# Fixed places for eight additions in a layer's opening, and a new order of its latent statistics

## The chip, the cores and the metric

The kernel runs on one core of one Trainium2 chip. The metric is the time of one execution on the device in microseconds. The kernel before took 889.29 us, the median of three runs (886.87, 889.29 and 890.32). One more execution was profiled: it took 887.62 us, and its profile spans 885.8 us of them.

The engines are named as in the profile: PE is TensorE (matmul), DVE is VectorE, ACT is ScalarE, POOL is GpSimd, SP is SyncE, which only issues transfers here.

## The reference

One decoder layer on x of 512 tokens by 2048, all in float32. Eight heads of latent attention (MLA) and eight forgetting heads (FoX) stand side by side behind one input projection.

```python
h = _rms_norm(x, g_pre)
proj = h @ w_in
(q_lat, kv_lat, k_rope_raw, gate_mla,
 fq, fk, fv, f_logit, gate_fox) = jnp.split(proj, split_points, axis=-1)
# MLA: q = rms_norm(q_lat) @ w_uq; k, v from rms_norm(kv_lat) @ w_ukv; rotary parts
# FoX: c = cumsum(log_sigmoid(f_logit + b_forget)); logits = q k * scale + c_q - c_k
o_mla = _mla_branch(q_lat, kv_lat, k_rope_raw, g_q, w_uq, g_kv, w_ukv, cos, sin) * jax.nn.silu(gate_mla)
o_fox = _fox_branch(fq, fk, fv, f_logit, b_forget) * jax.nn.silu(gate_fox)
o = jnp.concatenate([o_mla, o_fox], axis=-1) @ w_out
return x + _rms_norm(o, g_post)
```

The latents q_lat (768 wide) and kv_lat (512 wide) are normalised over their width, so each needs a sum of squares per token, a root, and a factor per token.

## The kernel before

**Precision.** Every float32 operand is held as two parts, hi (rounded) and lo (the rest), and a product is three matmuls: hi by hi, hi by lo, lo by hi (`mm3`, lines 152 to 154). Of x's tiles the parts are `hh` and `hl` ("h" in the profile). Of a weight they are `whi`, cast by ACT (line 290), and `wlo`, subtracted by DVE (line 291), for each chunk of up to 128 by 1024 numbers. The raw chunk is loaded by SP's queue (`raw`) or POOL's (`rawv`, `rawg`, `rawl`).

**Opening.** x comes in as tokens by width and is turned tile by tile (16 tiles of 128 columns): `x_turn(k)` (line 537) has four transposes on PE into one bank ("xt"), ACT's scaling for the hi part (line 144) and DVE's subtraction for the lo part (line 145). The loop of `proj_first` multiplies tile k with the first chunks of weights (line 655, banks "in"), two tiles to a chunk from the third chunk on. After tile k it turns the next ones: singly for k below 2, then two at a time after each even k. ACT also squares x here (line 550), for the norm of x. The opening is under a manual schedule: PE, ACT and DVE run what `proj_first` holds in the order in which it is written.

**Everything behind.** Outside of it a scheduler orders the instructions of each engine by its own estimate of when they can run; each engine then runs its list strictly in order. Side work (statistics, splits, copies, sums) stands in a queue `todo`, from which the loops over matmuls take a step now and then; `wait(n)` puts n empty steps into it.

**Sums of x.** Products are done in blocks after Strassen's manner, which need sums and differences of x's four quarters. `x_steps(j)` makes those of pair j of tiles (j = 0 to 3): four additions hh + hl into the buffers "xr" (line 1128), then, put at the head of `todo`, `away_steps`: subtractions "rmg" (line 1027), a split "smg", and stores "awaymg" to DRAM by POOL's queue. Later products fetch them ("bmg", SP's queue).

**Forget gates.** `forget_sums` yields steps `fs`. The last of them turn the rows ("rf"), copy them (line 852), scan them (line 858, "fz") and store the result: "c_dram", line 859, by SP's queue. The row of x's norm factors, `make_row(rrow)`, is two matmuls (lines 580, 581) and a copy (582); "fqr" (line 1142) are the first queries times that row.

**Latents.** `latent(i)` copies tile i of the latents and sums its squares (banks "la", "lg", "mg" are of the products that make them). `stats_steps(j)` makes the factors for j = 1 (kv) and j = 0 (q): `mean` (matmuls with ones, "lbk" and "lbq", line 1495), `root`, `steps` and `ends`. `latent_row` turns the factors into a row ("lrk", then the copy "ls"), with which the latents are scaled (line 1532) and split ("ln").

**Up products and heads.** The keys' and values' up product runs on sums of latents that `operand_steps("u", ...)` splits: "suq", "sug"; its banks are uA, uC, uB, uG. For each of four pairs of heads `mla_q` makes three banks mq, splits two of them (lines 141 and 142), copies the first 128 columns of both whole to "mw" by ACT (`whole_block`, line 126: the first block's scores are computed from whole float32), and rotates the third. `mla_k` does likewise for the keys (banks "mk"), which share banks in rotation with those of mq.

Of the kernel before, what the change touches and what calls it, by code (L numbers as in the profile page):

```python
# [19 lines left out]
P = 128  # L20
# [45 lines left out]
def tile_hybrid_layer(  # L66
# [39 lines left out]
    def proj_bank(name):  # L106
        return bank("pj", name, 4)
# [336 lines left out]
    for n in ("q0", "p1", "k0", "q6", "p2", "p4", "g7", "q1", "g5", "k1", "g3", "q2", "k2", "q3", "k3"):  # L444
# [5 lines left out]
        p = int(n[1])  # L450
# [181 lines left out]
    def proj_first(rng, banks):  # L632

        squares = deque(range(2 * NK))
        make_gcol(gains, 0, NK)
        x_turn(0, lambda: prepare(0))
        k = 0
        for i in rng:
            hi, lo = chunk(i, ahead=0)
            n = chunks[i][4]  # L640
            for j in range(chunks[i][3]):
# [19 lines left out]

                for turn in (k + 2,) if k < 2 else () if k % 2 else (k + 2, k + 3):
                    if turn < NK:
                        x_turn(turn)
                if k < 4 and k % 2 == 0:
                    prepare(rng[k // 2 + 2])
                for _ in range(3 if k > 2 and k % 2 else 2):
                    if squares:
                        x_square(squares.popleft())
                k += 1  # L670

# [447 lines left out]

    def x_steps(j):  # L1120

        pair = []

        def whole(h, i):
            if not pair:
                pair.extend(v_block(f"xr{n}{j}") for n in range(2))
            k = 2 * j + 8 * h + i
            dve.tensor_tensor(out=pair[h][:, i, :], in0=hh[k].bitcast(F32), in1=hl[k].bitcast(F32), op=ALU.add)
            if h and i:
                todo.extendleft(reversed(away_steps("m", j, pair, keep="g5")))  # L1130

        return [lambda h=h, i=i: whole(h, i) for h in range(2) for i in range(2)]


# [128 lines left out]
    def two_of(make, name):  # L1263
        return [make(f"{name}{i}") for i in range(2)]

    vb = [proj_bank(f"in{t}") for t in range(NT)]
    with tc.manual_schedule(engines={mybir.EngineType.Activation, mybir.EngineType.DVE, mybir.EngineType.PE}):
# [16 lines left out]
    wait(1)  # L1284
    todo.extend([*x_steps(0), *fs[3:], *x_steps(1)])
    places = [(g, j) for g in "vg" for j in range(4)]
# [5 lines left out]
    drain()  # L1292
    todo.extend([*x_steps(2), *x_steps(3)])

# [191 lines left out]
    def stats_steps(j):  # L1486
# [16 lines left out]

        def root():
            act.sqrt(w, v)

        def steps():
            dve.reciprocal(y, w)
            newton_rsqrt(y, v, w)
            if j == 0:  # L1510
                for to, scale in ((qcol, SC_M), (nqcol, -SC_M)):
                    dve.scalar_tensor_tensor(out=to, in0=y, scalar=scale, in1=rcol, op0=ALU.mult, op1=ALU.mult)
                return
            dve.tensor_tensor(out=y, in0=y, in1=rcol, op=ALU.mult)
# [4 lines left out]

        return [mean, root, steps, ends]  # L1520

# [56 lines left out]
    def first_latents():  # L1578
        wait(2)
        todo.extend(lambda i=i: latent(i, raw(i)) for i in (6, 7, 4, 5))  # L1580
        todo.extend(lambda i=i: latent_part(i) for i in (4, 5))
        todo.extend(s1)
        todo.append(lambda: latent_row(1))
        todo.extend(lambda i=i: latent_part(i) for i in range(6, 10))
# [17 lines left out]
    todo.extend(lambda i=i: latent(i, raw(i)) for i in range(4))  # L1602
    wait(3)
    todo.append(lambda: latent_stats(0))

# [17 lines left out]
    todo.append(lambda: k_parts.extend(zip(*(latents[i] for i in range(6, 10)))))  # L1623
    todo.extend(operand_steps("u", 0, (raws_of[4], raws_of[0]), ("sums",), tmp, part_slot))

# [17 lines left out]
    def mla_q(p):  # L1643

        qb = [proj_bank(f"mq{p}{i}") for i in range(3)]
        proj_T(mla[p]["q"], [(qb[i], P, cols(i * P)) for i in range(3)], qnh, qnl, 2, 6)
        q = [[split(qb[i], f"mq{p}{i}", first=P)] for i in range(2)]
        wholes = slot(f"mw{p}")
        qw = [[whole_block(wholes, i, qb[i])] for i in range(2)]
        a, b = rotate(qb[2], P, 1.0, f"q{p}")  # L1650
# [299 lines left out]
```

## Time and profile before

| | us |
|---|---|
| median of three runs | 889.29 |
| profiled execution | 887.62 |
| its span | 885.8 |
| PE busy | 874.8 |
| DVE busy | 628.6 |
| ACT busy | 503.3 |
| POOL busy | 125.2 |

A busy share says how full an engine is over the whole span; what a change of order is worth is read at the place where an engine waits. A row of the timeline gives start, duration (both in us), engine, line, operation, output and inputs, a shape, and how many like it stand together; in brackets stand the idle time just before it and what ended that. Two matmuls overlap in the pipe, so the distance of two starts, rather than a duration, is what one costs. PE's granted clock was 0.997 of full speed.

### The profile page before, as it was taken

To read this page: it belongs to the slowest core of one execution; us is meant where nothing else is said; L and a number is where in the kernel's file an instruction comes from. 1 tells how busy PE (TensorE), PEld (TensorE's weight loads), DVE (VectorE), ACT (ScalarE), POOL (GpSimd) and SP (SyncE) were. 2 spreads that over 40 slices of the span, in tenths; PEclk is the share of its full clock that TensorE was granted. 3 is DMA by queue.
4 is the path that set the end of the run, shared out by engine and by line. 5 is a ranking of instruction groups with operands and counts; after the bars stand their busy time and mean duration, and the time that the engine had idled before them with its cause. 6 is when DMAs were issued, how large, how long until landed. Compare 5 with 4: busy or idle time off the path is not lost.

```text
span 885.8 us, 13760 instructions
## 1 busy us (share of the span) xinstructions
PE 874.8 (99%) x5078; PEld 772.4 (87%) x5078; DVE 628.6 (71%) x1059; ACT 503.3 (57%) x919; POOL 125.2 (14%) x132
## 2 busy tenths in 40 slices
PE   9999999999999999999999999999999999999996
PEld 9989999999888888889999999988888788888885
DVE  4779466667475644547577677899778777988785
ACT  6844444444167553535654445649685986645383
POOL 0024004450110101000014432100000000000021
PEclk9999999999999999999999999999999999999998
DMA  9499869998597888884799999986969537699878
GB/s 295 146 356 241 274 196 202 228 229 228 87 214 213 223 209 234 228 233 125 248 306 229 236 216 252 207 225 158 222 146 274 121 133 248 203 330 321 260 216 250
DMA packets 128488, 198.41 MB, mean 224 GB/s; under 512 B 16338, under 2 KB 61292, under 8 KB 127396
## 3 DMA queue, kind: packets, MB, share of 16 engines
q1 hardware_dynamic: 101428, 136.28, 49.1%
q0 software_dynamic: 26256, 61.02, 35.2%
q8 instruction: 40, 0.66, 0.3%
q10 hardware_dynamic: 736, 0.22, 0.1%
q14 instruction: 28, 0.23, 0.1%
HBM read 182.60 MB, written 44.25 MB: 256 GB/s over the span
## 4 chain that ended last, share of the span: by engine, by line
PE 85%; DVE 6%; DMA 4%; ACT 3%; issue 1%; SPq 1%; DVEq 0%; ACTq 0%
PE fq L152 3%; PE fk L152 3%; PE fk L154 3%; PE fq L154 3%; PE fk L153 3%; PE fq L153 3%; PE in L655 3%; PE sm L698 2%; DVE wlo L291 2%; PE sf L698 2%; PE oa L153 2%; PE oa L154 2%; PE oa L152 2%; PE od L153 1%; PE od L154 1%; DMA rawl<-in_w_in_dram 1%
## 5 line engine op out<-in xcount | busy, mean ns | idle before, releaser
L291 DVE TENSOR_TENSOR wlo<-raw,whi 128x1024 fp32r<-128x1024 f32 (+3 forms) x159 | 186.7, 1176 | 95.8 <-ACT whi L290 94.6
L290 ACT CAST whi<-raw 128x1024 fp32r<-128x1024 f32 (+3 forms) x159 | 160.4, 1013 | 156.6 <-PE fk L153 43.2
L152 PE MATMUL fk<-h,whi 128*128 128x512 f32 x128 | 51.4, 401 | 0.0
L152 PE MATMUL fq<-h,whi 128*128 128x512 f32 x128 | 50.4, 394 | 0.0
L154 PE MATMUL fk<-h,wlo 128*128 128x512 f32 x128 | 50.1, 392 | 0.0
L154 PE MATMUL fq<-h,wlo 128*128 128x512 f32 x128 | 50.1, 391 | 0.0
L153 PE MATMUL fq<-h,whi 128*128 128x512 f32 x128 | 50.0, 391 | 0.0
L153 PE MATMUL fk<-h,whi 128*128 128x512 f32 x128 | 49.9, 390 | 0.0
L290 ACT CAST whi<-rawv 128x1024 fp32r<-128x1024 f32 x24 | 25.2, 1050 | 43.3 <-PE gg L153 11.0
L290 ACT CAST whi<-rawl 128x1024 fp32r<-128x1024 f32 x25 | 26.2, 1048 | 34.7 <-PE mc L153 7.9
L291 DVE TENSOR_TENSOR wlo<-rawl,whi 128x1024 fp32r<-128x1024 f32 x25 | 30.5, 1224 | 21.7 <-ACT whi L290 21.4
L291 DVE TENSOR_TENSOR wlo<-rawv,whi 128x1024 fp32r<-128x1024 f32 x24 | 29.3, 1224 | 23.1 <-ACT whi L290 23.1
L290 ACT CAST whi<-rawg 128x1024 fp32r<-128x1024 f32 x24 | 25.2, 1052 | 30.6 <-PE vc L154 8.4
L291 DVE TENSOR_TENSOR wlo<-rawg,whi 128x1024 fp32r<-128x1024 f32 x24 | 29.3, 1222 | 13.9 <-ACT whi L290 13.9
L1770 POOL DMA_DIRECT2D c<-in_x_dram x8 | 7.0, 1014 | 171.1 <-ACT c L1769 171.1
L718 ACT ACTIVATE pf<-pf,stf 128x128 f32<-128x128 f32 (+3 forms) x32 | 17.9, 559 | 22.5 <-DVE stf L709 22.5
L243 POOL DMA_DIRECT2D rawl<-in_w_in_dram x20 | 23.8, 1194 | 43.6 <-DVE wlo L291 32.0
L655 PE MATMUL in<-whi,h 128*128 128x328 f32 x128 | 29.1, 319 | 0.0
L152 PE MATMUL mq<-ln,whi 128*128 128x512 f32 x72 | 28.9, 402 | 0.0
L154 PEld LDWEIGHTS fk<-h,wlo 128*128 128x128 f32 x128 | 24.0, 188 | 5.3
L154 PEld LDWEIGHTS fq<-h,wlo 128*128 128x128 f32 x128 | 24.0, 188 | 5.2
L153 PE MATMUL mq<-ln,whi 128*128 128x512 f32 x72 | 28.2, 392 | 0.0
(628 smaller groups left out, 2916.1 us busy)
## 6 DMA issues: line engine op xcount, KB each, us to landing
raw<-in_w_in_dram SPq DMA_DIRECT2D x62, 512.0 KB
raw<-in_w_out_dram SPq DMA_DIRECT2D x32, 512.0 KB
rawl<-in_w_in_dram POOLq DMA_DIRECT2D x20, 512.0 KB, 11.3
rawv<-in_w_in_dram POOLq DMA_DIRECT2D x16, 512.0 KB, 8.1
rawg<-in_w_in_dram POOLq DMA_DIRECT2D x16, 512.0 KB, 8.8
raw<-in_w_in_dram POOLq DMA_DIRECT2D x12, 512.0 KB, 10.2
bmg<-awaymg SPq DMA_DIRECT2D x20, 256.0 KB
rawl<-in_w_in_dram SPq DMA_DIRECT2D x10, 512.0 KB
```

What stands on the lines that cost most here:

```text
L152: pe.matmul(o, ah, bh, start=first, stop=False, **kw)
L153: pe.matmul(o, ah, bl, start=False, stop=False, **kw)
L154: pe.matmul(o, al, bh, start=False, stop=last, **kw)
L243: pool.dma_start(to, second, accum_op=ALU.add)
L290: act.copy(hi[:, :m], raw[:, :m])
L291: dve.tensor_tensor(out=lo[:, :m], in0=raw[:, :m], in1=hi[:, :m].bitcast(F32), op=ALU.subtract)
L655: pe.matmul(banks[t][:, :n], a[k][:, tss[t]], b[:, j, :], start=k == 0 and m == 0, stop=k == NK - 1 and m == 2,)
L698: m = pe.matmul(s[:, :nn], a[:, qs], c[:, :nn], start=(i == 0), stop=(i == len(pairs) - 1))
L718: act.activation(p, p, AF.Exp, bias=st[:, 0:1], scale=unit, accum_out=st[:, 1:2])
L1770: pool.dma_start(to, x[piece(t, c)], accum_op=ALU.add)
```

## The change

It has four parts.

1. Opening: tiles 4 and 5 are turned singly (k below 4 instead of below 2), so that the sixth tile's transposes come after the next tile's matmuls.
2. The eight additions of pairs 0 and 1 (`x_wholes`) get fixed places in the manual schedule: one after each of tiles 10 to 13 and two after each of tiles 14 and 15, while the list lasts. Their sums (`x_sums`) stay in `todo`, both ahead; `x_steps(2)` follows them, ahead of the last forget steps `fs[3:]`, and only `x_steps(3)` is left for the next product.
3. Latent statistics: for kv one empty step moves from ahead of the latents to ahead of `latent_row`, and `root` is no step of its own any more; for q the statistics stand behind the first four steps of the "u" sums instead of three empty steps ahead of all of them.
4. `mla_q` copies each bank's first block to "mw" before it splits the bank, bank by bank, instead of after both splits.

```diff
     def proj_first(rng, banks):
         squares = deque(range(2 * NK))
+        wholes = deque(early_wholes)
...
-                for turn in (k + 2,) if k < 2 else () if k % 2 else (k + 2, k + 3):
+                for turn in (k + 2,) if k < 4 else () if k % 2 else (k + 2, k + 3):
                     if turn < NK:
                         x_turn(turn)
...
                     if squares:
                         x_square(squares.popleft())
+                if k > 9 and wholes:
+                    for _ in range(2 if k > 13 else 1):
+                        wholes.popleft()()
                 k += 1
...
-    def x_steps(j):
-
-        pair = []
+    x_pairs = {}
+
+    def x_wholes(j):
 
         def whole(h, i):
+            pair = x_pairs.setdefault(j, [])
             if not pair:
                 pair.extend(v_block(f"xr{n}{j}") for n in range(2))
             k = 2 * j + 8 * h + i
             dve.tensor_tensor(out=pair[h][:, i, :], in0=hh[k].bitcast(F32), in1=hl[k].bitcast(F32), op=ALU.add)
-            if h and i:
-                todo.extendleft(reversed(away_steps("m", j, pair, keep="g5")))
 
         return [lambda h=h, i=i: whole(h, i) for h in range(2) for i in range(2)]
+
+    def x_sums(j):
+        return [lambda: todo.extendleft(reversed(away_steps("m", j, x_pairs[j], keep="g5")))]
+
+    def x_steps(j):
+        return [*x_wholes(j), *x_sums(j)]
...
+    early_wholes = [*x_wholes(0), *x_wholes(1)]
...
-    todo.extend([*x_steps(0), *fs[3:], *x_steps(1)])
+    todo.extend([*x_sums(0), *x_sums(1), *x_steps(2), *fs[3:]])
...
-    todo.extend([*x_steps(2), *x_steps(3)])
+    todo.extend(x_steps(3))
...
-        def root():
+        def steps():
             act.sqrt(w, v)
-
-        def steps():
             dve.reciprocal(y, w)
...
-        return [mean, root, steps, ends]
+        return [mean, steps, ends]
...
     def first_latents():
-        wait(2)
+        wait(1)
         todo.extend(lambda i=i: latent(i, raw(i)) for i in (6, 7, 4, 5))
         todo.extend(lambda i=i: latent_part(i) for i in (4, 5))
         todo.extend(s1)
+        wait(1)
         todo.append(lambda: latent_row(1))
...
-    wait(3)
-    todo.append(lambda: latent_stats(0))
...
-    todo.extend(operand_steps("u", 0, (raws_of[4], raws_of[0]), ("sums",), tmp, part_slot))
+    sums = operand_steps("u", 0, (raws_of[4], raws_of[0]), ("sums",), tmp, part_slot)
+    todo.extend([*sums[:4], lambda: latent_stats(0), *sums[4:]])
...
-        q = [[split(qb[i], f"mq{p}{i}", first=P)] for i in range(2)]
         wholes = slot(f"mw{p}")
-        qw = [[whole_block(wholes, i, qb[i])] for i in range(2)]
+        q, qw = [], []
+        for i in range(2):
+            qw.append([whole_block(wholes, i, qb[i])])
+            q.append([split(qb[i], f"mq{p}{i}", first=P)])
```

The order in which DVE runs the opening around the fifth and sixth tile, before (h_284 and h_292 are these tiles' lo parts, wlo_296 is the lo part of the weights that both are multiplied with, wlo_337 that of the next two):

```order
L145 SCALAR_TENSOR_TENSOR h_260<-xt_255,gcol,h_260 128x512
L145 SCALAR_TENSOR_TENSOR h_284<-xt_279,gcol,h_284 128x512
L145 SCALAR_TENSOR_TENSOR h_292<-xt_287,gcol,h_292 128x512
L291 TENSOR_TENSOR wlo_296<-raw_142,whi_295 128x656
L291 TENSOR_TENSOR wlo_337<-raw_147,whi_336 128x656
```

and of the change (h_312 is the sixth tile now, wlo_288 its weights):

```order
L145 SCALAR_TENSOR_TENSOR h_260<-xt_255,gcol,h_260 128x512
L145 SCALAR_TENSOR_TENSOR h_284<-xt_279,gcol,h_284 128x512
L291 TENSOR_TENSOR wlo_288<-raw_142,whi_287 128x656
L145 SCALAR_TENSOR_TENSOR h_312<-xt_307,gcol,h_312 128x512
L291 TENSOR_TENSOR wlo_337<-raw_147,whi_336 128x656
```

The weights' lo part now stands ahead of the sixth tile's lo part.

DVE between the second and the third rawv's wlo, before (rawv_668 is the second rawv, rawv_670 the third; xr are the additions of pair 2):

```order
L852 COPY rf<-rf 72x512
L858 SCALAR_TENSOR_TENSOR fz<-rf,fz 8x512
L291 TENSOR_TENSOR wlo_824<-rawv_668,whi_823 128x1024
L1142 SCALAR_TENSOR_TENSOR fqr_867<-fq_676,rrow 128x512
L1128 TENSOR_TENSOR xr_891<-h_284 128x512
L1142 SCALAR_TENSOR_TENSOR fqr_867<-fq_677,rrow 128x512
L291 TENSOR_TENSOR wlo_881<-rawv_670,whi_880 128x1024
```

and of the change, right ahead of the third rawv's (rawv_682 here):

```order
L856 COPY rf<-rf 72x512
L1151 SCALAR_TENSOR_TENSOR fqr_882<-fq_688,rrow 128x512
L1151 SCALAR_TENSOR_TENSOR fqr_882<-fq_689,rrow 128x512
L862 SCALAR_TENSOR_TENSOR fz<-rf,fz 8x512
L291 TENSOR_TENSOR wlo_900<-rawv_682,whi_899 128x1024
L1133 TENSOR_TENSOR xr_910<-h_345 128x512
```

The copy rf and the scan fz have moved from ahead of the second rawv's wlo to right ahead of the third's, behind both fqr and, further up, behind the sums of pairs 1 and 2.

ACT at the last of the four pairs of heads, before (mq_7189 and mq_7190 are the pair's two query banks, mk_7408 its first key bank, boa and phm other work):

```order
L141 CAST mq_7386<-mq_7189 128x384
L141 CAST mq_7389<-mq_7190 128x384
L290 CAST whi_7412<-raw_7109 128x1024
L141 CAST boa_7105<-boa_7105 128x512
L126 COPY mw_7392<-mq_7189 128x128
L126 COPY mw_7392<-mq_7190 128x128
L141 CAST boa_7103<-boa_7103 128x512
```

and of the change:

```order
L126 COPY mw_7386<-mq_7189 128x128
L141 CAST mq_7388<-mq_7189 128x384
L126 COPY mw_7386<-mq_7190 128x128
L141 CAST mq_7392<-mq_7190 128x384
L290 CAST whi_7412<-raw_7109 128x1024
L141 CAST boa_7105<-boa_7105 128x512
L141 CAST boa_7103<-boa_7103 128x512
```

Both copies mw have moved up, ahead of the weight cast and the first boa cast, each in front of its bank's split.

## The prediction

> **What bounds the kernel now.** I read the page's head first, then the list of PE's waits.
>
> ```profile
> span 885.8 us, 13760 instructions
> PE 874.8 (99%) x5078; PEld 772.4 (87%) x5078; DVE 628.6 (71%) x1059; ACT 503.3 (57%) x919; POOL 125.2 (14%) x132
> ```
>
> TensorE is busy for 874.8 of 885.8 us, and no matmul is added or taken away: TensorE has the same work after the change. Only its idle time can move, and there are 11 us of it. The list of what PE waited for (total, times, longest, in us) splits them:
>
> ```profile
> PE mix L1795 <- ACT scaler L1794: 2.2, 1, 2.2
> PE warm L171 <- DVE warm L166: 1.1, 1, 1.1
> PE mk L152 <- ACT mw L126: 0.7, 1, 0.7
> PE in L655 <- DVE wlo L291: 0.6, 1, 0.6
> PE uC L152 <- ACT suq L141: 0.4, 1, 0.4
> ```
>
> The first two are the end and the start, which the change leaves alone. The other named waits are below 1 us each. Three of them stand where the change works: `in` (the opening), `uC` (the latent sums), `mk` (the head pair behind mla_q). So the question is what those three are worth, and whether reordering makes new ones.
>
> **The change, part by part.** The profiled execution took 887.62 us, its span and 1.8 us around it; the runs have a median of 889.29, which is 1.67 more. I work out the change in the span and apply it to the median.
>
> (a) *Fifth and sixth tile singly.* The stall of the opening, PE then ACT then DVE:
>
> ```profile
> 15.95 0.35 PE L655 MATMUL in<-whi,h 128*128 128x328 f32 x1
> 16.86 0.42 PE L655 MATMUL in<-wlo,h 128*128 128x328 f32 x1 [0.56 <-DVE wlo L291]
> 13.93 1.27 ACT L144 ACTIVATE h<-xt,gcol 128x512 fp32r<-128x512 f32 x2 [0.75 <-PE xt L540]
> 15.09 0.74 ACT L290 CAST whi<-raw 128x656 fp32r<-128x656 f32 x1
> 14.65 1.41 DVE L145 SCALAR_TENSOR_TENSOR h<-xt,gcol,h 128x512 fp32r<-128x512 f32 x2 [1.48 <-ACT h L144]
> 15.98 0.83 DVE L291 TENSOR_TENSOR wlo<-raw,whi 128x656 fp32r<-128x656 f32 x1
> ```
>
> Both halves' scalings stand ahead of the weight cast on ACT, and both halves' splits ahead of wlo on DVE; the matmul at 16.86 waits for that wlo (15.98 + 0.83 = 16.81). Normal pitch of such a matmul is 0.15, so 0.91 - 0.15 = 0.76 is lost. Afterwards only one scaling stands ahead: the cast starts half of 1.27, about 0.6, earlier (14.5), ends at 15.25, and wlo, behind one split (14.65 to 15.35), runs 15.3 to 16.14. PE wants it at about 16.1: **-0.68**. It could be -0.76 at best and 0 if the sixth tile, now transposed later, stalls the next step by as much.
>
> (b) *The eight additions and the steps moved behind them.* Before, the scheduler had put those additions into gaps of DVE's opening already; they move down by some 15 rows at most, and DVE is still through with them before its first subtraction of them. What costs is further on. Now both pairs' sums and x_steps(2) stand ahead of the forget gates' rows, so that four operations come right ahead of the third rawv's wlo: the copy rf, two fqr, the scan fz. Rows of DVE, then PE:
>
> ```profile
> 47.66 0.69 DVE L582 COPY rrow<-rrow 128x512 f32<-128x512 f32 x1
> 49.55 0.68 DVE L142 TENSOR_TENSOR smg<-rmg,smg 128x512 fp32r<-128x512 f32 x1
> 50.16 1.22 DVE L291 TENSOR_TENSOR wlo<-raw,whi 128x1024 fp32r<-128x1024 f32 x1
> 59.87 1.22 DVE L858 TENSOR_TENSOR_SCAN fz<-rf,fz 8x512 f32<-8x512 f32 x1
> 66.97 1.22 DVE L291 TENSOR_TENSOR wlo<-rawv,whi 128x1024 fp32r<-128x1024 f32 x1
> 42.85 0.40 PE L152 MATMUL fq<-h,whi 128*128 128x512 f32 x1
> 71.31 0.39 PE L153 MATMUL va<-wlo,h 128*128 128x512 f32 x1
> ```
>
> Before, that wlo is done at 68.19 and PE takes it at 71.31: 3.1 us of cover. Afterwards, with (a), PE takes it at 70.63. DVE's work up to it: the row rrow's second matmul now stands behind 35 rows of PE from 42.17 on (42.85 - 0.68), at 0.23 each, so it ends near 50.6, and the copy rrow can begin. From there to the copy rf stand 18 operations of 512 columns at a pitch of 0.61 (49.55 to 50.16), 10.9; three wlo at 1.14, 3.4; and twelve small ones with their waits on ACT, 2.1, an estimate: four of 128 columns take 0.88 in (d)'s first row, which makes 2.6 for twelve, and these are shorter: 67.0. Then rf and two fqr, 1.8, fz 1.2, wlo 1.2: done at 71.3 against 70.63. **+0.7**; 0 if the small ones take 1.4 or less, +1.5 if they and their waits take 2.9. Nothing else hides it: the wlo's cover of 3.1 is what the four operations and the sums ahead of them use up. Behind that wlo stand four more additions and the fourth rawv's wlo, which PE wants 12 matmuls later; DVE's rate there is unchanged, so no second wait is added.
>
> (c) *SyncE's queue.* The store of fz (c_dram) stands in SyncE's queue ahead of the next product's raw loads, and fz is now done near 70 rather than 61:
>
> ```profile
> 61.11 0.34 SPq L859 DMA_DIRECT2D c_dram<-fz  x1
> 61.55 23.76 SPq L255 DMA_DIRECT2D raw<-in_w_in_dram  x5
> 84.94 11.19 SPq L255 DMA_DIRECT2D raw<-in_w_in_dram  x4
> raw<-in_w_in_dram POOLq DMA_DIRECT2D x12, 512.0 KB, 10.2
> 82.39 1.05 ACT L290 CAST whi<-raw 128x1024 fp32r<-128x1024 f32 x1 [0.90 <-PE ga L153]
> 98.39 1.05 ACT L290 CAST whi<-raw 128x1024 fp32r<-128x1024 f32 x1 [3.64 <-DMA raw<-in_w_in_dram]
> 99.17 0.28 PE L154 MATMUL ga<-h,wlo 128*128 128x256 f32 x1
> 102.05 0.28 PE L154 MATMUL ga<-h,wlo 128*128 128x256 f32 x1
> ```
>
> Four loads go out at 61.55 and after; the fifth at 84.94. The first cast reads at 82.39, so loads that leave at 70.3 have 12 us, where such a load took 10.2 from POOL's queue: hidden, with 2 us to spare. The fifth also waits now for a store of x's last sums (awaymg); it is wanted by the matmul at 99.17, a cast and a wlo (1.05 + 1.22) earlier, 96.9. If it leaves three to four us later, at 88 or 89, it lands at 96 to 99 by 8 to 10 us. **+0.4**, between 0 and +1.5. The sixth stood as the late one before (cast at 98.39) and goes with an earlier store now.
>
> In a sentence that nothing else needs: the Trainium skill, "DMA: Bandwidth & Descriptors", in "Anatomy of one DMA — SWDGE (gpsimd) path", has it that a semaphore wait holds up the issuing sequencer, not the DMA engines. By that rule the four loads can't pass c_dram, and the raw row at 61.55, 0.44 behind c_dram's at 61.11, agrees; were the rule wrong, (c) would be 0.
>
> (d) *Latent statistics.* One pump step fewer stands ahead of the row lrk, and the split of lat comes earlier than one wlo. DVE, PE:
>
> ```profile
> 560.75 0.88 DVE L572 TENSOR_SCALAR lrkdl<-ident,lrkl 128x128 fp32r<-128x128 f32 x4
> 562.76 0.39 PE L581 MATMUL lrk<-lrkdl,ones 128*128 128x512 f32 x1
> 572.26 1.21 DVE L291 TENSOR_TENSOR wlo<-raw,whi 128x1024 fp32r<-128x1024 f32 x1
> 573.40 0.74 DVE L1532 SCALAR_TENSOR_TENSOR lat<-lat,gcol,ls 128x512 f32<-128x512 f32 x1
> 573.53 0.38 PE L154 MATMUL mg<-bmg,wlo 128*128 128x256 f32 x1
> ```
>
> The second lrk matmul goes 12 matmuls (of 0.12) earlier, 561.3, while its operand ends at 561.63: +0.2 after the first has taken its time. The wlo that ends at 573.47 is wanted at 573.53; with the lat scaling (0.66) ahead of it instead of behind, less what DVE gained by an earlier row, it is about 0.5 late. Together **+0.7**, 0 to +1.2.
>
> (e) *latent_stats(0) behind the first four sums.* The splits of suq and sug come forward, ahead of queries' latent work.
>
> ```profile
> 601.36 0.50 PE L152 MATMUL uC<-whi,suq 128*128 128x512 f32 x1 [0.36 <-ACT suq L141]
> 602.78 0.73 PE L154 MATMUL uC<-whi,suq 128*128 128x512 f32 x2 [0.22 <-DVE suq L142]
> 600.69 0.62 ACT L141 CAST suq<-ruq 128x512 fp32r<-128x512 f32 x1
> ```
>
> uC twice waits for suq, whose cast ran only at 600.69. With both operands made before the last queries' matmuls both waits go, with the refill behind each (start to start 0.52 and 0.40): **-0.9**; 0 if the operand is late for another reason, -1.1 if the next sums' operands gain as well.
>
> (f) *mla_q: copy ahead of split.*
>
> ```profile
> 702.50 0.47 PE L154 MATMUL mk<-ln,wlo 128*128 128x512 f32 x1
> 703.66 0.50 PE L152 MATMUL mk<-ln,whi 128*128 128x512 f32 x1 [0.69 <-ACT mw L126]
> 703.35 0.47 ACT L126 COPY mw<-mq 128x128 f32<-128x128 f32 x2
> 702.50 1.02 DVE L142 TENSOR_TENSOR mq<-mq,mq 128x384 fp32r<-128x384 f32 x2
> ```
>
> The keys' new bank is free once both copies mw have read it; they stood on ACT behind a weight cast and a boa cast. The last read becomes DVE's split (702.50, first half done near 703.0), so PE goes on at about 703.0: **-0.7**. The order of the softmax and the output products around it changes too, since the scheduler planned them anew: between -1.2 and +0.3.
>
> Sum: -0.68 + 0.7 + 0.4 + 0.7 - 0.9 - 0.7 = **-0.5 us**, 0.06%: 888.8 for the median, 888.7 taken; the 0.1 is rounding down towards the gains, whose causes are the plainer ones. The bounds add to -3.1 (-0.76 - 1.1 - 1.2) and to +4.5 (1.5 + 1.5 + 1.2 + 0.3).
>
> **Rivals.** 0.5% of the time, 4.4 us, is about what a measurement of this kernel can tell from no change.
>
> *Gains without new waits.* If DVE and SyncE absorb (b), (c), (d), what is left is -0.68 - 0.9 - 0.7 = -2.3, up to -3.1: **887** to 886.2. For it: DVE is busy 71% and each new wait is below 1 us by my working, with 0 among its bounds. Against: the wlo at 573.53 had 0.06 us of cover. Still within 0.5%.
>
> *SyncE's queue decides (the other side).* The fifth raw load waits for a store that lands as late as the sixth's did (its cast came at 98.39, having waited 3.64 for the load). If the store holds the fifth by 10 us, to 94.9 (the three issues behind it in its row ended at 96.13), and it takes 10.2, it lands at 105.1, its wlo is done at 107.4, and the matmul of 99.17 waits 8.2 us: 889.3 - 0.9 (the sum without (c)) + 8.2 = **897**, slower by 0.8%. It decides from a landing behind 96.9, and passes 4.4 us at a landing behind 101.3. For it: one head of one queue holds all loads behind it. Against: the last sums are made earlier on DVE than before, so their store should leave earlier.
>
> *Nothing shows.* The additions were in the opening anyhow, and a gain at 16, 601 or 703 is taken back at a later spot where PE waits for a load that has its own time: **889.3**. For it: the late matmuls above wait for splits of loads, and a load's time doesn't follow PE's. Against: only one cast above, the one at 98.39, waited for its load.
>
> **How the numbers follow.** The forecast, new small waits eating small gains, 0.50 (0.03 of it beyond 0.5% on the faster side and 0.02 on the slower, for stages that the scheduler planned anew and I don't cost); gains without new waits 0.25 (0.05 of it beyond 0.5%, if part of the other idle time goes too); nothing shows 0.15; SyncE's queue 0.10, half of it past 4.4 us. So faster 0.03 + 0.05 = 0.08, slower 0.02 + 0.05 = 0.07, and 0.85 between. The range runs from the bound of the gains, 886.2, less 0.7 for the spread of medians, to the upper bound short of SyncE's full price, 889.3 + 3.2: 885.5 to 892.5.
>
> **What would show it.** (a): no PE wait at 15.95. (b): a new PE wait for a wlo near 70.6, of 0.5 to 1.5, with fz's scan ending near 70. (c): c_dram's issue near 70, the loads right behind; no wait before 96. (d): PE waits at 561 and 573 below 1 us. (e), (f): uC and mk without their waits. Wrong would be: a PE idle stretch above 2 us anywhere between 70 and 110, or a stage that is shorter by more than its PE wait was.

## The result

The changed kernel took 891.79 us (median of 17 runs, 890.55 to 894.03), the kernel before beside it 889.41 us (17 runs, 886.87 to 892.64). The ratio is 1.0027, with a 95% interval of 1.0018 to 1.0037: slower by 2.4 us, clear of zero, and inside the half per cent that the prediction called no change. The prediction had 888.7 us, so the sign is wrong. The time lies in the range.

The head of the changed kernel's page, and its list of what TensorE waited for (total, times, longest, in us; smaller rows left out):

```profile
span 890.4 us, 13770 instructions
PE 876.0 (98%) x5078; PEld 772.5 (87%) x5078; DVE 628.7 (71%) x1059; ACT 502.3 (56%) x919; POOL 125.1 (14%) x132
```

```profile
PE mix L1805 <- ACT scaler L1804: 2.2, 1, 2.2
PE uB L152 <- ACT u L1731: 1.5, 1, 1.5
PE warm L171 <- DVE warm L166: 1.1, 1, 1.1
PE ga L152 <- ACT whi L290: 0.8, 1, 0.8
PE ga L154 <- DVE wlo L291: 0.8, 1, 0.8
PE oa L152 <- ACT whi L290: 0.7, 1, 0.7
PE sm L702 <- ACT mw L126: 0.6, 1, 0.6
PE va L153 <- DVE wlo L291: 0.4, 1, 0.4
```

The work is the same, 5078 matmuls. The old waits `in`, `uC` and `mk` are gone from the list, as predicted, and six new ones stand in it: `va` (forecast), two at `ga` (forecast far too small), `uB`, `oa` and `sm` (not forecast).

To see where the time goes, I matched each matmul of a run with the same one of the first profile of before and took the median of how much later it starts, stage by stage. A *loss* below is a distance of two starts beyond the usual one of such a pair; it is a little more than the wait in the list, since the pipe has to fill again.

| stage (us of before) | what changed there | predicted | shift so far | step |
|---|---|---|---|---|
| up to 42 | (a) opening | -0.68 | -0.78 | -0.8 |
| 42 to 95 | (b) va | +0.7 | -0.10 | +0.7 |
| 95 to 105 | (c) ga | +0.4 | +1.95 | +2.05 |
| 105 to 552 | none | 0 | +1.95 | 0 |
| 552 to 625 | (d), (e), uB | -0.2 | +4.08 | +2.1 |
| 625 to the end | (f) mk, oa, od | -0.7 | +4.64 | +0.6 |

By profiles the change costs 4.6 us, by medians 2.4. The two profiles differ by more than the medians because the first profile of before is a favourable execution (887.62 us against a median of 889.41; only two of the 17 runs were shorter), while that of the changed kernel, 892.13 us, is close to its median.

The third rawv's wlo (VectorE, then TensorE), where the prediction expected the wait:

```profile
69.79 1.23 DVE L291 TENSOR_TENSOR wlo<-rawv,whi 128x1024 fp32r<-128x1024 f32 x1
71.07 0.50 PE L153 MATMUL va<-wlo,h 128*128 128x512 f32 x1 [0.40 <-DVE wlo L291]
```

SyncE's and GpSimd's queues, ScalarE's casts and TensorE between 69 and 102 us:

```profile
69.78 0.35 SPq L863 DMA_DIRECT2D c_dram<-fz  x1
70.23 23.39 SPq L255 DMA_DIRECT2D raw<-in_w_in_dram  x8
78.94 0.58 POOL L1021 DMA_DIRECT2D awaymg<-rmg  x1
90.93 2.69 SPq L255 DMA_DIRECT2D raw<-in_w_in_dram  x4
90.88 1.05 ACT L290 CAST whi<-raw 128x1024 fp32r<-128x1024 f32 x1 [1.33 <-PE va L154]
98.66 1.05 ACT L290 CAST whi<-raw 128x1024 fp32r<-128x1024 f32 x1 [6.72 <-DMA raw<-in_w_in_dram]
99.76 0.38 PE L152 MATMUL ga<-h,whi 128*128 128x256 f32 x1 [0.76 <-ACT whi L290]
101.02 0.39 PE L154 MATMUL ga<-h,wlo 128*128 128x256 f32 x1 [0.76 <-DVE wlo L291]
```

c_dram goes at 69.78 and the first four raw loads right behind it; the row of 90.93 is the other four of the eight, seen in a narrower window. The store awaymg of 78.94 lands at 90.78; the fifth load leaves at 90.93, six us later than in the kernel before, and ScalarE sits idle for 6.72 us before it can cast it. TensorE then waits twice, for the hi part and for the lo part, and loses 2.05 us.

What SyncE's queue waited for at these stores (total, times, longest, in us), before and then changed:

```profile
SPq L255 <- DMA awaymg<-rmg: 9.3, 2, 9.1
SPq L255 <- DMA awaymg<-rmg: 19.3, 2, 18.5
```

Before, such a store held the sixth load for 9.1 us (it left at 94.59); now one holds the fifth for 18.5 us.

The second product uB (ScalarE, then TensorE):

```profile
620.22 1.00 ACT L724 ACTIVATE pm<-pm,stm 128x256 f32<-128x256 f32 x2
621.31 0.56 ACT L1731 COPY u<-uA 128x512 f32<-128x512 f32 x1
621.93 0.50 PE L152 MATMUL uB<-whi,ln 128*128 128x512 f32 x1 [1.46 <-ACT u L1731]
```

In the kernel before the first of the two copies that free uA's banks ran ahead of softmax work, and PE was never held there:

```profile
614.43 0.56 ACT L1721 COPY u<-uA 128x512 f32<-128x512 f32 x1
```

Now both copies (621.31 and 622.59) stand behind more of the softmax steps of `pm`, and uB, which takes over a bank of uA, waits.

### The profile page after: what moved, and what is told of

It is laid out like the page before. It is cut to its first block, busy times and chain, and to the rows that moved or that the text cites. A ratio compares the mean times of both kernels' runs of the same rounds, so it can differ in the third digit from the quotient of the medians.

```text
span 890.4 us, 13770 instructions
## 1 busy us (share of the span) xinstructions
PE 876.0 (98%) x5078; PEld 772.5 (87%) x5078; DVE 628.7 (71%) x1059; ACT 502.3 (56%) x919; POOL 125.1 (14%) x132
## 4 chain that ended last, share of the span: by engine, by line
PE 81%; DVE 7%; DMA 5%; ACT 5%; issue 1%; DVEq 0%; ACTq 0%; SPq 0%; POOLq 0%
PE fk L152 3%; PE fk L154 3%; PE fk L153 3%; DMA rawl<-in_w_in_dram 3%; PE fq L152 2%; PE fq L153 2%; PE fq L154 2%; PE in L656 2%; PE mq L152 2%; PE sm L702 2%; PE sf L702 2%; PE mq L153 2%; PE mq L154 2%; DVE wlo L291 2%; PE oa L154 2%; PE oa L153 2%
## 5 line engine op out<-in xcount | busy, mean ns | idle before, releaser
L291 DVE TENSOR_TENSOR wlo<-raw,whi 128x1024 fp32r<-128x1024 f32 (+3 forms) x159 | 186.7, 1176 | 99.3 <-ACT whi L290 96.8
L152 PE MATMUL mq<-ln,whi 128*128 128x512 f32 x72 | 29.1, 404 | 0.0
L154 PE MATMUL mq<-ln,wlo 128*128 128x512 f32 x72 | 28.3, 392 | 0.0
```

The lines of the kernel that those rows point to most:

```text
L152: pe.matmul(o, ah, bh, start=first, stop=False, **kw)
L154: pe.matmul(o, al, bh, start=False, stop=last, **kw)
L291: dve.tensor_tensor(out=lo[:, :m], in0=raw[:, :m], in1=hi[:, :m].bitcast(F32), op=ALU.subtract)
```

## The experiments

Two questions: what makes the 2.05 us at 98 to 101, and what makes uB late. Then: does any part gain, and why do profiles and medians differ. All ratios are to the kernel before, run on the same chip beside them, with 11 or 12 runs of each experiment.

| run | median us | ratio (95%) | span | shift at 75-95 | at 105-130 | at 625-700 | at 840-870 |
|---|---|---|---|---|---|---|---|
| changed | 891.79 | 1.0027 (1.0018 to 1.0037) | 890.4 | -0.10 | +1.95 | +4.08 | +4.64 |
| forget steps first | 890.35 | 1.0013 (1.0004 to 1.0022) | 888.8 | +0.04 | +1.05 | +2.79 | +3.11 |
| c_dram by GpSimd | 890.41 | 1.0016 (1.0007 to 1.0025) | 887.8 | +0.45 | +0.69 | +1.83 | +2.09 |
| kv statistics as before | 890.37 | 1.0013 (1.0002 to 1.0025) | 890.5 | +0.16 | +2.05 | +3.98 | +4.78 |
| q statistics as before | 889.90 | 1.0007 (0.9999 to 1.0016) | 887.7 | +0.19 | +2.11 | +1.66 | +1.97 |
| single turns alone | 888.58 | 0.9997 (0.9986 to 1.0009) | 889.1 | -0.34 | -0.34 | +3.23 | +3.29 |
| copies alone | 888.64 | 1.0001 (0.9990 to 1.0013) | 887.3 | +0.19 | +0.19 | +1.39 | +1.63 |
| sums and forget as before | 889.37 | 1.0005 (0.9994 to 1.0016) | 887.0 | -0.60 | -0.60 | +0.46 | +1.14 |
| root a step again | 887.47 | 0.9988 (0.9979 to 0.9996) | 885.5 | -0.92 | -0.92 | -0.45 | -0.12 |
| the same, copies as before | 887.44 | 0.9985 (0.9973 to 0.9997) | 884.5 | -1.08 | -1.08 | -1.35 | -1.33 |
| kv statistics alone | 888.04 | 0.9986 (0.9977 to 0.9995) | 887.2 | +0.04 | +0.04 | +1.22 | +1.60 |

The ratios come from all runs, the shifts from one profiled execution each. The intervals of the first three experiments overlap with that of the changed kernel; the others lie clear of it.

**The forget steps first, on the changed kernel.**

```diff
-    todo.extend([*x_sums(0), *x_sums(1), *x_steps(2), *fs[3:]])
+    todo.extend([*x_sums(0), *fs[3:], *x_sums(1), *x_steps(2)])
```

> The changed kernel, but with the last forget steps put back ahead of the sums of pair 1, so that the scan fz and its store c_dram run near 61 us instead of 70; everything else, also the rotation of buffers by which the fifth raw load waits for a store of x's last sums, stays. In the changed kernel PE loses 2.05 us at 98 to 101 us (waits for whi, then wlo, of the fifth load). Theory A (head of SyncE's queue: the four loads held behind c_dram to 70 us collide with POOL's fills and stores, the store that releases the fifth load lands late): the loss at 98 to 101 falls below 0.5 us, c_dram is issued near 62 and the total falls by 1.6 to 2.0 us against the changed kernel. Theory B (the fifth load is late only because its buffer is now one that a store must leave first): the loss stays at 1.7 to 2.3 us and the total stays within 0.4 us. In both the wait of 0.7 us near 70 us stays, since as many operations stand ahead of the third rawv's wlo on VectorE.

SyncE's queue, the fifth load's cast and TensorE:

```profile
64.43 0.35 SPq L863 DMA_DIRECT2D c_dram<-fz  x1
97.76 1.05 ACT L290 CAST whi<-raw 128x1024 fp32r<-128x1024 f32 x1 [5.69 <-DMA raw<-in_w_in_dram]
100.13 0.39 PE L154 MATMUL ga<-h,wlo 128*128 128x256 f32 x1 [0.75 <-DVE wlo L291]
```

Neither theory holds alone. c_dram goes 5.3 us earlier, the loads with it, and the loss falls from 2.05 to 1.0 us, half of it. The wait at va, which both theories kept, went (VectorE now has the scan elsewhere), but the transposes rf wait 0.3 us instead, so the step between 42 and 95 stays near +0.5.

**c_dram from GpSimd's queue, on the changed kernel.**

```diff
-            nc.sync.dma_start(c_dram, total)
+            pool.dma_start(c_dram, total)
```

> The changed kernel with the one store c_dram issued from GpSimd's queue instead of SyncE's; no other order changed on VectorE. Theory A (SyncE's queue head holds the raw loads): the first raw loads leave between 61 and 71 us each as its own buffer comes free, the store of x's last sums lands before 88, and the loss of 2.05 us at 98 to 101 falls below 0.8 us. Theory B (the buffer's store decides, whatever the queue): the loss stays at 1.7 us or more. A third possibility, C: GpSimd, now waiting for fz itself, issues its fills of rawv later and the third or fourth rawv comes late: a new wait between 72 and 80 us.

SyncE's queue and the fifth load's cast on ScalarE:

```profile
59.14 33.18 SPq L255 DMA_DIRECT2D raw<-in_w_in_dram  x8
97.39 1.05 ACT L290 CAST whi<-raw 128x1024 fp32r<-128x1024 f32 x1 [4.91 <-DMA raw<-in_w_in_dram]
```

The first loads leave from 59 us on, and the loss at 98 to 101 is 0.24 us, below the bound that theory A gave. But ScalarE still waits 4.91 us for the fifth load: the same store gates it and lands at 89.47, not before 88 as theory A had it, so the load leaves at 89.6 instead of 90.9. Part of the gain is that TensorE itself was 0.5 us later here, by a wait of 1.0 us for x in the opening. No new wait stands between 72 and 80.

**Sums and forget steps as before, the additions still fixed.**

```diff
-    todo.extend([*x_sums(0), *x_sums(1), *x_steps(2), *fs[3:]])
+    todo.extend([*x_sums(0), *fs[3:], *x_sums(1)])
...
-    todo.extend(x_steps(3))
+    todo.extend([*x_steps(2), *x_steps(3)])
```

> The changed kernel with the eight additions still in their fixed places, but the side work behind the opening in the order of before: sums of pair 0, forget steps, sums of pair 1, then pairs 2 and 3 in the next product. The fifth raw load then waits for VectorE again and not for a store. The putting back of the forget steps alone left 1.05 us of the 2.05 us at 98 to 101. Theory A (that remainder is the fifth load's wait for the store of x's last sums): the losses at 70 and at 98 to 101 are both below 0.2 us, the total 2.5 to 2.8 us below the changed kernel. Theory B (the remainder comes from the fixed places of the additions or from the single turns, by which PE comes to these loads earlier): 0.5 us or more stay at 98 to 101.

The fifth and the sixth load's casts:

```profile
93.09 1.05 ACT L290 CAST whi<-raw 128x1024 fp32r<-128x1024 f32 x1 [1.67 <-PE va L154]
96.33 1.05 ACT L290 CAST whi<-raw 128x1024 fp32r<-128x1024 f32 x1 [2.18 <-DMA raw<-in_w_in_dram]
```

The fifth cast waits for TensorE to give a buffer back, not for its load: the load left at 84.1. Nothing is lost at 98 to 101, so theory A holds for what was left. The ratio falls from 1.0027 to 1.0005. Of the step between 42 and 95 0.5 us stays, as a wait of rf.

So the 2.05 us have one condition: the fifth load's buffer is one that a store of x's last sums must leave first, and without the condition nothing is lost. The store takes 10 to 12 us to land (78.94 to 90.78 here, 79.06 to 89.88 with the forget steps first, 79.49 to 89.47 with c_dram on GpSimd's queue). It landed sooner in the two profiles whose first loads leave earlier, but such a store also took 13.3 us with loads at 63 to 66 (82.88 to 96.13 with sums and forget steps as before), so why it takes so long, and why it landed sooner there, stays open.

The size follows from the landing. By the prediction's chain a load that lands at 96.9 is just in time for TensorE as it ran before; adding each profile's own shift at 75 to 95, the fifth cast was 1.9 us late in the changed kernel (98.66 against 96.8), 0.8 with the forget steps first (97.76 against 96.94) and 0.04 with c_dram on GpSimd's queue (97.39 against 97.35). The losses were 2.05, 1.0 and 0.24: each the lateness and about 0.2 us more.

**kv statistics as before, on the changed kernel** (two empty steps ahead, `root` a step of its own).

```diff
-        return [mean, steps, ends]
+        return [mean, root, steps, ends]
...
-        wait(1)
+        wait(2)
         todo.extend(lambda i=i: latent(i, raw(i)) for i in (6, 7, 4, 5))
         todo.extend(lambda i=i: latent_part(i) for i in (4, 5))
         todo.extend(s1)
-        wait(1)
         todo.append(lambda: latent_row(1))
```

> The changed kernel with the kv statistics (empty steps, root) as before the change; the place of the q statistics and all else as changed. In the changed kernel the stretch 555 to 577 loses 1.06 us (lrk's two matmuls and mg's wlo) and the second uB product waits about 2.3 us near 621 us for a copy of uA that ScalarE runs behind softmax work. Theory A (the late copy is the scheduler's answer to both edits of the statistics together: with this one undone, it puts the copy back ahead of a softmax exponential): both losses go, 3.0 to 3.4 us less than the changed kernel, and the gain at uC (1.26 us) stays. Theory B (moving the q statistics alone makes the copy late, since it sits on ScalarE in the same stretch): only the 1.06 us go, the wait at uB stays above 1.5 us.

The first copy of uA, which has its old place among the exponentials again (TensorE runs 4.0 us later here than in the first profile of before, where the copy stood at 614.43):

```profile
618.38 0.56 ACT L1732 COPY u<-uA 128x512 f32<-128x512 f32 x1
```

The wait at uB is gone: theory A there. But the span didn't fall. In place of the waits at lrk came 1.10 us in mg near 576, where the first profile of before loses nothing, and a wait of 0.8 us in lbq, where it waits 0.4. That was the first sign that this stage differs between executions.

**q statistics as before, on the changed kernel.**

```diff
+    wait(3)
+    todo.append(lambda: latent_stats(0))
...
-    todo.extend([*sums[:4], lambda: latent_stats(0), *sums[4:]])
+    todo.extend(sums)
```

> The changed kernel with the q statistics where they were (behind three empty steps, ahead of all sums); the kv edit stays. Theory A (both edits together make the copy of uA late): the 2.3 us at uB go, the gain of 1.26 us at uC goes too (uC waits again for suq, 0.5 to 0.9 us), the loss of 1.06 us in 555 to 577 stays: about 1.0 us less than the changed kernel. Theory B (the kv edit alone makes the copy late by its shift of VectorE's list): the wait at uB stays, and the total is 0.9 to 1.3 us above the changed kernel.

uB's wait is gone here as well, and uC waits again (0.58 us lost). So each of the two edits alone leaves the copies in place; only both together move them back behind the exponentials. Through lrk's two matmuls 0.35 us were lost, less than expected (0.79 in the changed kernel), and mg lost nothing.

**Single turns alone, on the kernel before.**

```diff
-                for turn in (k + 2,) if k < 2 else () if k % 2 else (k + 2, k + 3):
+                for turn in (k + 2,) if k < 4 else () if k % 2 else (k + 2, k + 3):
```

> The kernel before with tiles 4 and 5 turned singly and nothing else changed. Theory A (the prediction's step a): the stall of 0.76 us at 15.95 us goes and nothing comes in its place, so the profiled matmuls from 20 us on stand 0.5 to 0.8 us earlier than in the kernel before up to the end, ratio about 0.9993. Theory B (a later place where PE waits for loads takes it back): the gain of 0.5 to 0.8 us is gone again by 120 us or by 700 us.

The stall at 15.95 is gone, and half of it was lost again to a wait of 0.5 us for x at 8 us, which other profiles have too, 0.2 to 1.0 us long, with and without the single turns. From 105 to 552 the gain of 0.34 us (0.23 at the end of it) stays. Then 3.5 us are lost between 552 and 610, although all three engines run there just what the kernel before runs. This execution (890.85 us) is the longest of the 12. In the ratio the gain can't be told from nothing.

**Copies alone, on the kernel before** (mla_q's part of the change).

```diff
-        q = [[split(qb[i], f"mq{p}{i}", first=P)] for i in range(2)]
...
+            qw.append([whole_block(wholes, i, qb[i])])
+            q.append([split(qb[i], f"mq{p}{i}", first=P)])
```

> The kernel before with only mla_q's order changed (copy mw ahead of each split). Theory A (the prediction's step f): the wait of mk near 702.5 falls from 0.93 us lost to 0.4 or less, no new wait elsewhere, total 0.5 to 0.7 us less. Theory B (the scheduler's new order of the last pair gives it back): a wait of 0.7 to 0.9 us for whi stands in oa near 716, as in the changed kernel near 721.5, and the total is within 0.3 us of the kernel before.

A row of its list of TensorE's waits:

```profile
PE oa L152 <- ACT whi L290: 0.7, 1, 0.7
```

mk loses 0.38 us instead of 0.93. In the output product oa 0.84 us are lost to a cast that comes late, where before 0.36 us were lost near it. Theory B: what is gained at mk is given back one product on.

**The kernel before, profiled again, and the changed one again.**

> The kernel before, profiled once more. Its first profile lost nothing in mg near 573 us and 0.35 us or less in lbq; the kernel with single turns alone, whose lists for TensorE, VectorE and ScalarE are the same as those of the kernel before from 40 us on, lost 1.2 us in mg and 2.1 us around lbq, behind loads (rawl, through GpSimd's queue) that landed 1.1 us later. Theory A (those waits belong to the kernel before too, and its first profile was a favourable execution): a loss of 0.5 to 1.2 us in mg near 573 us and 0.4 to 1.3 us in lbq, span 886.5 to 889. Theory B (the single turns bring the waits): no loss above 0.3 us there, span within 0.6 us of 885.8.

> The changed kernel, profiled once more, to see which of its losses repeat. Theory A (the losses at 70, 98 to 101, 604 and 621 come from the order of instructions and buffers): 0.4 to 0.7, 1.5 to 2.3, 0.5 to 0.9 and 1.5 to 1.7 us again at these places, whatever the loads near 555 to 577 do. Theory B (one of them is spread of one execution): it is below 0.3 us now.

The second profile of before took 892.36 us with a span of 890.6 us, 4.8 more than its first, and all of it lies between 552 and 610 us. Its waits at mg and lbq on TensorE's timeline, and then one window of 2 us behind them (length, then the busy time of PE, PEld, DVE, ACT and POOL, granted clock, DMA share, GB/s):

```profile
574.74 0.39 PE L154 MATMUL mg<-bmg,wlo 128*128 128x256 f32 x1 [0.92 <-DVE wlo L291]
591.71 1.52 PE L1495 MATMUL lbq<-ones,ls 128*128 128x1 f32 x8 [1.66 <-DVE ls L1477]
```

```profile
593.00:595.00 2.00, 2.00 (x7) 1.61 (x7) 0.84 (x3) 0.00 (x0) 0.00 (x0) 0.50 0.97 309
```

So theory A: these waits belong to the kernel before, though its span lies above the 889 that theory A allowed, by the slower clock. They begin with loads (rawl) on GpSimd's queue, some of which leave when an earlier one has landed: those landing at 550.04, 558.05 and 561.91 in the first profile landed at 551.18, 559.19 and 563.12 in the second, and within 0.2 us of these later times with the single turns alone and with the copies alone. Why they land later is not shown. From there ScalarE's cast and VectorE's list run 1.1 us later, mg, which had 0.06 us of cover, waits, and lbq waits 1.66 us instead of 0.4. From 592.1 us on, inside lbq, the granted clock is 0.50 for 6.8 us; up to 598.8 a matmul of 512 columns costs 0.43 us instead of 0.23.

How often the clock falls can be read from the runs, each of which has its mean granted clock on record. Of 65 runs of before on three of the chips (35, 15 and 15), 18 show 0.993 to 0.996 and the others 0.997 or more; the median of the 18 is 1.2 to 2.4 us longer, by chip. Of the runs of the single turns alone 5 of 12 are such, of the copies alone 2 of 12, of the other versions in the table, the changed kernel included, 1 of 107. So the second profile of before is no usual execution either: 892.36 us is longer than all 15 runs beside it (887.64 to 891.76). The copies alone, profiled at 889.07 near their median of 888.64, stand between the two: 1.11 us more at mg and 0.38 at lbq than the first profile of before, and no slow clock.

The changed kernel's losses came back at 70 (0.6 us), at 98 to 101 (1.9), at 605 (0.6) and at 621 (1.6): they come from the order, as theory A had it. In its second profile lrk waited more, and lbq not at all. From its list of waits:

```profile
PE lrk L580 <- ACT lrkdh L571: 1.2, 1, 1.2
```

**The root as its own step, additions and side work as before**, the rest as changed; in a second version mla_q's copies are as before too. On the changed kernel:

```diff
-                if k > 9 and wholes:
-                    for _ in range(2 if k > 13 else 1):
-                        wholes.popleft()()
...
-    todo.extend([*x_sums(0), *x_sums(1), *x_steps(2), *fs[3:]])
+    todo.extend([*x_steps(0), *fs[3:], *x_steps(1)])
...
-    todo.extend(x_steps(3))
+    todo.extend([*x_steps(2), *x_steps(3)])
...
-        return [mean, steps, ends]
+        return [mean, root, steps, ends]
```

> A version to be better than both: single turns, copies ahead of splits, q statistics behind the first four sums, the kv edit with its empty steps moved but the root still a step of its own; additions, sums and forget steps all as before the change. In the scheduler's list for ScalarE one copy of uA then stands ahead of the softmax exponentials again. Theory A (the late copies came only from the merged step's shift by one slot, and the loads at 98 only from the reordered side work): no wait at uB above 0.3 us, none at 70 or 98, the gain at uC stays (0.9 to 1.3 us) and the losses in 555 to 577 stay (0.5 to 1.1 us): 0.5 to 1.2 us below the kernel before. Theory B (any shift of this stage puts a similar wait somewhere in 604 to 660): a new loss of 1 us or more there, total at or above the kernel before.

> The version with the root as its own step, but with mla_q's copies as before the change. Theory A (the copies' order gives as much as it takes: 0.55 us at mk against 0.5 us in oa): within 0.4 us of that version, ratio to the kernel before 0.998 to 0.9995, with a loss of 0.9 us at mk near 702 and none of 0.84 us in oa. Theory B (the copies' order loses through the earlier stage, where sm waits for mw 1.0 us near 602): the wait of sm near 602 goes, and the total is 0.8 us or more below that version.

Both are faster than both kernels: 0.9988 and 0.9985 of the kernel before, so by the ratios 3.5 to 3.7 us below the changed kernel. Of the second, the two waits that are left in the middle of its list:

```profile
PE sm L698 <- ACT mw L126: 1.1, 1, 1.1
PE mk L152 <- ACT mw L126: 0.7, 1, 0.7
```

No wait at uB, ga, va or lbq in either: theory A of the first version, and of the second too, since the copies' order makes no difference between the two. With sums and forget steps as before but root merged (the third experiment) the wait at uB was 1.5 us. So the merged root, together with the moved q statistics, makes uB late, as far as these tell: the fixed additions differ between the two as well. The 12 runs of the first lie between 886.70 and 888.54; of the 35 of the kernel before beside it 21 took longer than the longest of these, up to 891.81. The faster version is also the steadier one, as it would be without the waits at lbq: none of its 12 runs shows a granted clock below 0.997, and 8 of those 35 do.

**kv statistics alone, on the kernel before.**

> The kernel before with the kv statistics' edit alone (one empty step moved behind the statistics, root merged into the next step). In the three profiles with this stage's order of before (the second profile of the kernel before, the single turns alone, the copies alone) TensorE lost 1.1 to 1.2 us in mg near 573 us and about 1.0 to 2.1 us around lbq near 590 us; in those with this edit it lost 0 to 0.4 us at mg, nothing at lbq, and 0.3 to 1.7 us at the row lrk near 563 us. Theory A (the edit removes the waits at mg and lbq, being a gain in the usual execution though the first profile of before shows neither): mg below 0.5, lbq below 0.2, uC's waits as before, ratio to the kernel before 0.997 to 0.9995. Theory B (the waits at lrk give it back): lrk loses 1 us or more and the total is within 0.4 us of the kernel before.

0.9986: a gain of 1.2 us by itself, though its one profile, the second longest of the 11 runs, loses 1.75 us through lrk's two matmuls. Theory A holds by the ratio and by mg and lbq, where nothing is lost. Of B one half held, the loss at lrk; the other, a total within 0.4 us of before, did not. The slow clock alone isn't the gain: the 11 of the 15 runs of before at 0.997 or more have a median of 888.90, still 0.9 us above 888.04. How the gain splits between mg, lbq and lrk in a usual execution is not shown.

## Why the prediction was wrong

- **What bounds the kernel** was right: TensorE's work is the same in every run, and all of the time lies in a handful of waits.
- **(a)** -0.68 forecast, -0.8 measured. Right: the stall is gone in every profile with the single turns. By the wait for x at 8 us the shift behind the opening varies from -0.24 to -1.09 in these.
- **(b)** +0.7 forecast, +0.7 measured (0.40 us of wait and the refill); the wlo was done at 71.0, forecast 71.3. The sum over VectorE's list held. The eight fixed additions themselves cost nothing that the runs show.
- **(c)** is the step that failed by its size: "+0.4, between 0 and +1.5" against 2.05 (1.9 in the second profile). The mechanism was named, a fifth load that waits for a store. The term that was mis-sized is that load's leaving: "at 88 or 89", but the store took 11.8 us to land and the load left at 90.93. Its cast began at 98.66, inside the 96 to 99 that the prediction gave for the landing, because the load took 8 us or less, the short end of its "8 to 10": a lucky offset. And the price did not follow from that landing: against its own 96.9, a landing at 99 is 2.1 us late, more than the upper bound of 1.5, and +0.4 is the price of one near 97.3. TensorE's two waits are two parts of the one lateness. The rival "SyncE's queue decides" was nearer than its chance of 0.10 said, with a quarter of its price. Undoing the order of the side work, and with it (c) and the wait of (b), takes back most of the slowdown (1.0027 to 1.0005).
- **uB** stands in no term. It is the other step that failed: stages that the scheduler planned anew got 0.05 of the chances and nothing in the sum. 1.6 us were lost there in both profiles, and with either edit of the statistics undone they are not. The lists of the changed kernel show the two copies behind more softmax steps; a bank that the next product takes over is the thing to look for in such a list.
- **(d)** +0.7 forecast. In the first pair of profiles 0.79 us were lost through lrk's two matmuls and 0.43 at mg, 1.2 together, and 0.56 came back at lbq, which the prediction doesn't mention: the agreement of the sum, +0.7, is luck. And the sign is wrong for the runs: the same edit alone makes the kernel faster (0.9986). Its profiles lose nothing at lbq and at most 0.43 us at mg; those of before's order lose more at both in three of four cases.
- **(e)** the waits of uC went, as forecast, and 0.58 to 0.76 us are lost instead at the scores sm, which wait for a copy mw behind it.
- **(f)** -0.7 forecast; 0.55 was gained at mk, and 0.5 was given back in oa. In the first profile some 0.6 us more went in spots of 0.3 us or less each, 0.27 of it at the product od near 795; in the second, where od lost nothing more than before, the whole stretch cost 0.24 us instead of 0.56. The bounds named the possibility (up to +0.3); the value was taken from the half that was easy to see.

In sum: -0.8 + 0.7 + 2.05 + 2.1 + 0.6 = +4.6 against one profile. That profile is 1.8 us shorter than the median of before (887.62 against 889.41) and that of the changed kernel 0.3 longer than its own, which leaves 2.5, near the measured 2.4. The stage where before varies is 552 to 625: three further profiles with its order there have +4.84, +3.46 and +1.41, two of them with the slow clock that 18 of 65 runs show, where the five profiles with the changed order have 1.2 to 2.7. So that stage is little or no loss on average, as an estimate from so few profiles: uB's 1.6 us stand against the 1.2 us that the kv edit gains by itself. What remains are the opening's order, (a), (b) and (c), and (f).

## What to carry to other kernels

When side work is reordered, follow the buffers as well as the queues: the load here was late because its buffer had become one that a store must leave first, and its price is how far its landing lies behind the latest one that TensorE doesn't notice. Where a scheduler plans a stage anew, read its new lists for the copies that free a bank before pricing the stage at zero. And take more than one profile of the kernel before: a margin of 0.06 us in one execution was a wait of about 1 us in three others, and an edit that looks like a loss beside it can be a gain.

## What was new about the hardware

A short wait can go with a loss of the clock. In the second profile of before TensorE waited 1.66 us and then ran eight matmuls of one column (591.71 to 593.09). The granted clock fell to 0.50 inside these eight, at 592.1, 2.0 us after the last full matmul ended, and stayed there for 6.8 us. With 1.29 us of waiting ahead of the same eight (the single turns alone) it fell at 592.8, 0.7 us after full matmuls were running again, and for 3.4 us. With 0.71 us (the copies alone) it stayed at 1.00. A wait of 1.46 us at uB, with full matmuls on both sides, left the clock at 1.00 too. Windows of the second profile of before, of the single turns alone, and of the changed kernel around uB's wait (columns as above):

```profile
591.50:592.00 0.50, 0.29 (x3) 0.33 (x3) 0.50 (x2) 0.00 (x0) 0.00 (x0) 1.00 0.73 98
592.10:598.80 6.70, 6.70 (x20) 5.44 (x20) 3.34 (x10) 2.08 (x5) 0.08 (x1) 0.50 0.81 210
```

```profile
592.15:592.75 0.60, 0.60 (x4) 0.52 (x5) 0.53 (x3) 0.00 (x0) 0.00 (x0) 1.00 0.60 232
593.00:595.00 2.00, 2.00 (x6) 1.61 (x5) 0.57 (x3) 0.59 (x2) 0.00 (x0) 0.50 1.17 248
```

```profile
619.00:623.00 4.00, 2.54 (x12) 1.79 (x11) 1.88 (x6) 4.00 (x12) 0.86 (x1) 1.00 0.96 294
```

What the one-column matmuls do to the clock was not tried by itself. The Trainium skill, "TensorE: Matmul & The Clock Gate", in "Part 1: The HAM clock gate (the "warmup" mystery)", puts the drop to half rate behind an idle window of about 3.4 us. These rows do not fit an idle stretch of that length: even with the eight small matmuls counted as idle, TensorE had been quiet for 2.0 us at the drop in the one case, and for 2.2 us in all (589.94 to 592.12) in the other.
